# Reading the mixer's projection input as two runs of 128 tokens in turn

## The chip, the cores and the metric

The kernel runs on one core of one Trainium2 chip. A core has a matrix engine (TensorE, here PE, with its weight loads shown apart as PEld), a vector engine (VectorE, DVE), an activation engine (ScalarE, ACT), a general engine (GpSimd, POOL) and a queue engine that issues transfers (SyncE, SP). Each works through its own instructions in order. The metric is the device time of one execution in microseconds; lower is better. Three runs of the kernel before took 1980.0, 1980.95 and 1983.24 us, the median is 1980.95.

## What is computed

One decoder layer in float32 for 256 tokens of width 2048: a feed-forward block (SwiGLU, inner width 5632), a token mixer, a second feed-forward block, and a final norm. Each is normed and modulated by a conditioning vector. The change lies in the mixer, whose projection is one large product with `w_in`:

```python
def hybrid_mixer(h, w_in, w_out, ...):
    proj = (h @ w_in).astype(jnp.float32)
    q_f, k_f, v_f, f_f, qkv_g, a_g, b_g, z_g = jnp.split(proj, SPLIT_IDX, axis=-1)
    logf = jax.nn.log_sigmoid(f_f + fox_f_bias)            # forget gates
    o_f = forgetting_attention(heads(q_f), heads(k_f), heads(v_f), logf)
    qkv_g = jax.nn.silu(causal_dwconv(qkv_g, gdn_conv))    # 4 taps along the tokens
    q_g, k_g, v_g = jnp.split(qkv_g, 3, axis=-1)
    o_g = gated_delta_rule(l2norm(q_g), l2norm(k_g), v_g, g_log, beta)
    ...
    return o @ w_out
```

There are 8 heads of forgetting attention ("fox") and 8 heads of the gated delta rule ("gdn"), each of width 128.

## The kernel before

**Precision.** A float32 product is made of three faster ones: weights and activations are each split into a high part and a rest, and high x high, high x rest and rest x high are summed in PSUM. For weights, ACT casts the high part (`whi`, line 109) and DVE subtracts it from the raw block for the rest (`wlo`, line 121). Weights come in blocks of eight 128x128 tiles, 512 KB each, in the order of use (`Stream`, lines 84 to 130), with three buffers each for the raw block, `whi` and `wlo`. So the cast of a block waits until PE has done with the block three before it.

**Layout of the activations.** The normed input `hs` has, for each of 16 slices of 128 features, a rest and a high part of 256 tokens. Two views of it are used. `part` (line 331) is for the feed-forward blocks: tokens are stored as two runs (even and odd tokens, written through `pairs`), and the matmul reads one element of the one and one of the other run in turn, which gives the tokens in order. `plain` (line 329) is for the mixer: 256 tokens in order, contiguous. `woven` (line 74) is the helper that reads a contiguous stretch as two halves in turn.

**The mixer's projections.** `project` (line 717) makes one or several outputs of 128 features x 256 tokens. It runs over 16 slices and makes three matmuls for each weight tile (lines 725 to 727) with `plain` as the moving operand. There are 41 such outputs: one for the gates, 24 for gdn (keys, queries, values), 16 for fox queries and keys. `project_rows` (line 731) is another form, with the activations as the stationary operand, for the fox values and the output gate `z`.

**What reads the sums.** `gates` (line 755) copies 24 rows out of PSUM (758), and works out decays in steps: exponentials on ACT, a series on DVE, cumulative sums on PE (800 to 809), then a copy (811) and a transfer of the rows to memory, from which they are read again spread over the partitions. `conv_silu` (line 871) makes the four-tap convolution: tap 3 on ACT (874), the others on DVE (876), with the sums read from PSUM each time, then a SiLU on ACT (877). It runs 24 times, with temporary tiles from the tag `pt`, which has four buffers (line 418). The fox queries and keys are taken out of PSUM by ACT at line 1192.

**Order.** The per-head work (`keys`, `decays`, `solve`, `gdn`, `fox`, `to_out`) is written as generators, and `tick` (line 433) advances them between the weight tiles at due times. A scheduler then sets the order of the instructions on each engine from these, so an edit in one place can move others. The list `ORDER` (line 49) sets which head's projection comes when; the first call projects the gates and three key heads together.

Of the kernel before, what the change touches and what calls it, by code (L numbers as in the profile page):

```python
# [12 lines left out]
AF = mybir.ActivationFunctionType  # L13
ALU = mybir.AluOpType
# [4 lines left out]
T = 256  # L19
KD = D // P  # L20
# [6 lines left out]
HD = 128  # L27
# [46 lines left out]
def woven(ap):  # L74

    return ap.rearrange("p (a b) -> p b a", a=2)


def pairs(ap):

    return ap.rearrange("p (b a) -> p b a", a=2)


class Stream:
# [49 lines left out]
def layer_kernel(ctx: ExitStack, tc: tile.TileContext, xrow, c, adaw, cols, cst, w, out, order, dbg=None):  # L134
    nc = tc.nc
    V, A, G, PE = nc.vector, nc.scalar, nc.gpsimd, nc.tensor
# [21 lines left out]
    def psn(i, name):  # L158

        i %= 8  # L160
        return psb(name) if i < N_BIG else pss(name) if i < N_BIG + N_GDN else psf(name)
# [165 lines left out]
    LO, HI = 0, 1  # L327

    plain = hsf[:, : KD * HS].rearrange("p (k i) -> p k i", k=KD)[:, :, : 2 * T].rearrange("p k (q t) -> p k q t", q=2)
# [78 lines left out]
    def h_need(k):  # L408

        h_upto(k + AHEAD)  # L410
# [6 lines left out]
    def pt(name):  # L417
        return tmp.tile([P, T], F32, name=name, tag="pt", bufs=4)
# [14 lines left out]
    def tick(us):  # L433
        clock["now"] += us
        for kind in chains:
            if chains[kind] and clock["now"] >= due[kind]:
                advance(kind)
# [248 lines left out]
    def mixer():  # L686
# [12 lines left out]
        R = slice(0, GR)  # L699
# [17 lines left out]
        def project(items):  # L717

            pp = [psn(i, "pp") for i in range(len(items))]
            todo = [(i, k) for k in range(KD) for i in range(len(items))]  # L720
            for i, k in todo:
                m, n = items[i]
                h_need(k)
                wh, wl = W.next(m, k, n)
                PE.matmul(pp[i][:, :T], wh, plain[:, k, HI], start=(k == 0), stop=False)  # L725
                PE.matmul(pp[i][:, :T], wh, plain[:, k, LO], start=False, stop=False)  # L726
                PE.matmul(pp[i][:, :T], wl, plain[:, k, HI], start=False, stop=(k == KD - 1))  # L727
                tick(TILE_US)
            return [p_[:, :T] for p_ in pp]

# [24 lines left out]
        def gates(ps):  # L755

            yr = x[:, 8]
            A.copy(yr[R], ps[R])
            y, ny, e, em, t0, q = (x[:, j, : 2 * GR].rearrange("p (t r) -> p t r", t=2) for j in range(10, KD))
            coef = tiny.tile([P, GR + PAD["hid"]], F32, name="coef", bufs=1)[:, :GR]  # L760
            tc.keep_in_program_order(A.activation(coef, L("alog"), AF.Exp))
            V.tensor_scalar(coef, coef, -1.0, None, ALU.mult)
            yield 1.0
            pc = psf("pcol")
            pcv = pc[:, : 2 * GR].rearrange("p (t r) -> p t r", t=2)
            for t in range(2):
                PE.transpose(pcv[:, t], yr[R, t * P : (t + 1) * P], ident[R, :GR])
            both = lambda c_: c_.unsqueeze(1).to_broadcast([P, 2, GR])
            V.tensor_tensor(y, pcv, both(L("gbias")), ALU.add)
            V.tensor_tensor(y, y, both(C("sgn")), ALU.mult)  # L770
            V.scalar_tensor_tensor(ny, y, -1.0, y, ALU.mult, ALU.min)
            A.activation(e, ny, AF.Exp)
            V.tensor_scalar(em, y, 0.0, None, ALU.min)
            A.activation(em, em, AF.Exp)

            S = ny
            V.tensor_scalar(t0, e, 2.0, None, ALU.add)
            V.reciprocal(t0, t0)
            V.tensor_tensor(S, e, t0, ALU.mult)
            V.tensor_tensor(t0, S, S, ALU.mult)  # L780
            V.tensor_scalar(q, t0, 1.0 / 17.0, None, ALU.mult)
            for n in (15, 13, 11, 9, 7, 5, 3):
                V.scalar_tensor_tensor(q, q, 1.0 / n, t0, ALU.add, ALU.mult)
            V.scalar_tensor_tensor(q, q, 1.0, S, ALU.add, ALU.mult)
            V.tensor_scalar(y, y, 0.0, None, ALU.max)
            V.scalar_tensor_tensor(y, q, 2.0, y, ALU.mult, ALU.add)
            V.tensor_tensor(y, y, both(coef), ALU.mult)

            V.tensor_scalar(t0, e, 1.0, None, ALU.add)
            V.reciprocal(t0, t0)  # L790
            V.tensor_tensor(colS[:, :, 4], em[:, :, 16:24], t0[:, :, 16:24], ALU.mult)
            yield 6.0

            fox_, gdn_ = slice(0, NH), slice(NH, 2 * NH)
            pr = psf("prow")
            po = psf("pcum")
            pcs = po[:, : 6 * NH].rearrange("p (t q r) -> p t q r", t=2, q=3)
            for t in range(2):
                sl = slice(t * P, (t + 1) * P)
                PE.matmul(pr[:NH, T + t * P : T + (t + 1) * P], y[:, t, gdn_], C("tri64"), start=True, stop=True)  # L800
                PE.matmul(pr[:NH, sl], y[:, t, fox_], C("tri"), start=True, stop=(t == 0))
                if t:
                    PE.matmul(pr[:NH, sl], y[:, 0, fox_], L("ones"), start=False, stop=True)
            for t in range(2):
                PE.matmul(pcs[:, t, 1], C("tri64"), y[:, t, gdn_], start=True, stop=True)
                PE.matmul(pcs[:, t, 2], C("tru64"), y[:, t, gdn_], start=True, stop=True)
                PE.matmul(pcs[:, t, 0], C("tri"), y[:, t, fox_], start=True, stop=(t == 0))
                if t:
                    PE.matmul(pcs[:, t, 0], L("ones"), y[:, 0, fox_], start=False, stop=True)
            rt = x[:, 8:10].rearrange("p a t -> p (a t)")[:NH]  # L810
            A.copy(rt, pr[:NH])
            nc.sync.dma_start(rows, rt)
            V.tensor_copy(colS[:, :, 0:2], pcs[:, :, 0:2])
            A.activation(colS[:, :, 2:4], pcs[:, :, 1:3], AF.Exp)
            V.tensor_tensor(nbeg, colS[:, :, 4], colS[:, :, 2], ALU.mult)
            V.tensor_scalar(nbt, colS[:, :, 4], -1.0, None, ALU.mult)
            V.tensor_scalar(ng, colS[:, :, 1], -1.0, None, ALU.mult)
            yield 2.0
            fetch_rows(0)
            yield 1.0  # L820
# [48 lines left out]
            G.memset(t_, 0.0)  # L869

        def conv_silu(ps, n, dst):
            cv = pt("cv")
            tap = lambda s: L("conv", 4 * n + s, 1)
            A.activation(cv, ps, AF.Copy, scale=tap(3))
            for s in range(1, 4):
                V.scalar_tensor_tensor(cv[:, s:], ps[:, : T - s], tap(3 - s), cv[:, s:], ALU.mult, ALU.add)
            A.activation(dst, cv, AF.Silu)

        kk = {}
# [277 lines left out]
        def step(kind, h):  # L1157
            if kind == "K":
                have_keys(h, project([("qkv", NH + h)])[0])
            elif kind == "G":  # L1160
                rowg[h] = row_of(h, 1, "g")
                pq = project([("qkv", h)])[0]
                pv = project([("qkv", 2 * NH + h)])[0]
                finish("gdn", h - 3)
                finish("out", h - 3)
                finish("k", h // 4 * 4 + 3)
                qv[h] = otile("qv")
                conv_silu(pq, h, qv[h].bitcast(F32)[:, 0])
                conv_silu(pv, 2 * NH + h, qv[h].bitcast(F32)[:, 1])
                ups[h] = decay(h)  # L1170
                start("gdn", h, gdn(h))
            elif kind == "Z":
                if h:
                    finish("fox", 3)
                pz = project_rows("z", h)
                zss[h] = [spare(0), spare(2)] if h else [m1p.tile([P, 512], F32, name=f"zs{t}") for t in range(2)]
                for t in range(2):
                    A.activation(zss[h][t], pz[t], AF.Silu)
            elif kind == "V":
                if h:  # L1180
                    finish("k", NH)
                pv = project_rows("vf", h)
                vts[h] = [spare(4 * h), spare(4 * h + 2)]
                for t in range(2):
                    A.copy(vts[h][t], pv[t])
            else:
                rowf[h] = row_of(h, 0, "f")
                pp = [project([(m, h)])[0] for m in ("qf", "kf")]
                finish("fox", h - 1)
                qk = spare(8 + 2 * (h % 2)).rearrange("p (a t) -> p a t", a=2)  # L1190
                for i in range(2):
                    A.activation(qk[:, i], pp[i], AF.Copy, scale=1.0 / math.sqrt(HD) if i == 0 else 1.0)
                start("fox", h, fox(h, qk, vts[h // 4]))

        first = project([("gt", 0)] + [("qkv", NH + h) for h in range(3)])
# [168 lines left out]
```

## Time and profile before

| | |
|---|---|
| Median of three runs | 1980.95 us |
| Profiled execution | 1983.29 us |
| Span of its instructions | 1981.5 us |
| Mean granted TensorE clock | 0.991 |
| PE busy | 1919.3 us (97%) |
| DVE busy | 1582.2 us (80%) |
| ACT busy | 1045.7 us (53%) |
| Matmuls in `project` | 1968 (lines 725, 726, 727, 656 each) |
| First and last of them | from 753.3 to 1166.6 us |

All lines of the profile come from the one profiled execution. A row of a group has: line, engine, operation, output <- input, sizes, count | busy time in us, mean ns of one | idle time of its engine just before, and what ended most of it. A row of the timeline has the start in us, the duration in us, engine, line, operation, count, and in brackets the idle time before it with what ended that. Neighbouring instructions of one kind are merged there. A row of waits has: who waited, on whom: total us, times, longest. Matmuls overlap: the next one starts before the one before it has ended, so a sum of durations is more than the time they take.

### The profile page before, as it was taken

The numbers are of one execution on the slowest core, as the hardware profiler recorded it, in microseconds if no ns is written. First come the engines' busy times: TensorE is split into PE (matmuls) and PEld (weight loads), VectorE is DVE, ScalarE is ACT, GpSimd is POOL, SyncE is SP. The second block draws the span as 40 slices with busy tenths as digits, with TensorE's granted clock in tenths as the row PEclk, the third lists the DMA queues.
The fourth block names the chain that finished last, engine by engine and source line by source line (L and its number), as shares of the span: only waits on it lengthen the run. The fifth ranks groups of instructions, "written<-read, shape, count | busy, mean of one in ns | idle before, by whom it ended". The sixth has DMA issues, their size and how long they took to land.

```text
span 1981.5 us, 33632 instructions
## 1 busy us (share of the span) xinstructions
PE 1919.3 (97%) x13059; PEld 1783.2 (90%) x13059; DVE 1582.2 (80%) x2424; ACT 1045.7 (53%) x1607; POOL 64.2 (3%) x60
## 2 busy tenths in 40 slices
PE   8999999999999999999999999999999999999997
PEld 6999999988999988889989998989999999999996
DVE  6999988999999998879878879987677666666665
ACT  6544555433555447666656656565454445555442
POOL 0000000000000120000000002000000000000012
PEclk8999999999999999999999999999999999999998
DMA  9989867999999984776666658667777555555563
GB/s 341 350 329 333 297 213 261 393 376 382 355 343 359 340 328 173 248 237 230 210 240 241 210 213 308 234 222 251 250 240 258 203 202 198 204 200 200 201 200 117
DMA packets 129489, 519.56 MB, mean 262 GB/s; under 512 B 18217, under 2 KB 21545, under 8 KB 111153
## 3 DMA queue, kind: packets, MB, share of 16 engines
q1 hardware_dynamic: 129330, 517.42, 72.6%
q8 instruction: 102, 1.67, 0.3%
q14 instruction: 57, 0.47, 0.1%
HBM read 512.89 MB, written 4.47 MB: 261 GB/s over the span
## 4 chain that ended last, share of the span: by engine, by line
PE 66%; DVE 14%; DMA 10%; issue 6%; ACT 4%; SPq 0%; DVEq 0%; ACTq 0%
PE pd L455 12%; PE pg L451 9%; PE pu L451 9%; PE pd L456 6%; DVE wlo L121 6%; DMA adat<-in_ada_dram 5%; PE pu L452 5%; PE pg L452 5%; DMA wraw<-in_w_dram 4%; PE pgu L539 3%; PE pgu L538 3%; PE pgu L537 3%; PE pp L725 2%; PE pp L727 2%; PE pp L726 2%
## 5 line engine op out<-in xcount | busy, mean ns | idle before, releaser
L121 DVE TENSOR_TENSOR wlo<-wraw,whi 128x1024 fp32r<-128x1024 f32 x674 | 820.6, 1226 | 238.2 <-ACT whi L109 236.0
L109 ACT CAST whi<-wraw 128x1024 fp32r<-128x1024 f32 x674 | 699.5, 1047 | 507.0 <-DMA wraw<-in_w_dram 195.0
L455 PE MATMUL pd<-hid,whi 128*128 128x512 f32 x1408 | 462.1, 382 | 0.8 <-DVE hid L470 0.8
L456 PE MATMUL pd<-hid,wlo 128*128 128x256 f32 x1408 | 384.6, 273 | 3.0 <-DVE wlo L121 3.0
L242 DVE CUSTOM_DVE_ANT_0 adat<-adat,cs,colt 128x2048 f32<-128x2048 f32 x140 | 329.0, 2350 | 52.6 <-DMA adat<-in_ada_dram 52.2
L451 PE MATMUL pg<-hs,whi 128*128 128x512 f32 x912 | 303.8, 384 | 3.9 <-ACT whi L109 2.8
L451 PE MATMUL pu<-hs,whi 128*128 128x512 f32 x912 | 302.6, 382 | 0.0
L455 PEld LDWEIGHTS pd<-hid,whi 128*128 128x128 f32 x1408 | 266.0, 189 | 38.0 <-DVE hid L470 1.4
L456 PEld LDWEIGHTS pd<-hid,wlo 128*128 128x128 f32 x1408 | 270.5, 192 | 5.9 <-DVE wlo L121 5.7
L537 PE MATMUL pgu<-hs,whi 128*128 128x256 f32 x896 | 245.9, 277 | 8.4 <-ACT hs L341 6.7
L452 PE MATMUL pu<-hs,wlo 128*128 128x256 f32 x912 | 249.9, 274 | 0.5 <-DVE wlo L121 0.3
L452 PE MATMUL pg<-hs,wlo 128*128 128x256 f32 x912 | 249.6, 274 | 0.0
L539 PE MATMUL pgu<-hs,wlo 128*128 128x256 f32 x896 | 244.6, 277 | 3.6 <-DVE wlo L121 3.5
L538 PE MATMUL pgu<-hs,whi 128*128 128x256 f32 x896 | 245.9, 276 | 0.1
L451 PEld LDWEIGHTS pg<-hs,whi 128*128 128x128 f32 x912 | 173.2, 190 | 28.6 <-issue 3.0
L725 PE MATMUL pp<-hs,whi 128*128 128x256 f32 x656 | 189.9, 291 | 4.2 <-ACT whi L109 1.4
L451 PEld LDWEIGHTS pu<-hs,whi 128*128 128x128 f32 x912 | 172.4, 189 | 23.6
L727 PE MATMUL pp<-hs,wlo 128*128 128x256 f32 x656 | 186.8, 286 | 1.6 <-DVE wlo L121 1.6
L726 PE MATMUL pp<-hs,whi 128*128 128x256 f32 x656 | 186.2, 284 | 0.0
L537 PEld LDWEIGHTS pgu<-hs,whi 128*128 128x128 f32 x896 | 172.4, 193 | 9.6 <-ACT hs L341 7.1
L452 PEld LDWEIGHTS pu<-hs,wlo 128*128 128x128 f32 x912 | 175.2, 192 | 3.2 <-DVE wlo L121 2.6
L452 PEld LDWEIGHTS pg<-hs,wlo 128*128 128x128 f32 x912 | 176.0, 193 | 0.4
(334 smaller groups left out, 2629.9 us busy)
## 6 DMA issues: line engine op xcount, KB each, us to landing
wraw<-in_w_dram SPq DMA_DIRECT2D x674, 512.0 KB, 4.5
adat<-in_ada_dram SPq DMA_DIRECT2D x140, 1024.0 KB, 7.3
xr<-in_xr_dram SPq DMA_DIRECT2D x4, 512.0 KB, 6.3
adaf<-in_ada_dram SPq DMA_DIRECT2D x4, 512.0 KB, 8.6
adaf<-in_ada_dram SPq DMA_DIRECT2D x2, 1024.0 KB, 12.2
xd<-x SPq DMA_DIRECT2D x4, 512.0 KB, 8.3
rw<-rowd SPq DMA_DIRECT2D x16, 128.0 KB, 6.4
x<-xd SPq DMA_DIRECT2D x4, 512.0 KB, 8.5
```

What stands on the lines that cost most here:

```text
L109: self.cast = self.nc.scalar.copy(self.h, r).ins
L121: nc.vector.tensor_tensor(self.l, r, self.h.bitcast(F32), ALU.subtract)
L242: V.tensor_tensor_reduce(t, t, cs, 1.0, L("adab", q, 1), ALU.mult, ALU.add, mod[:, q : q + 1])
L451: PE.matmul(ps, wt[0], both, start=(k == 0), stop=False)
L452: PE.matmul(ps[:, T:], wt[1], part(k, HI), start=False, stop=(k == KD - 1))
L455: PE.matmul(ps, wt[0], act.rearrange("p q (a b) -> p q b a", a=2), start=first, stop=False)
L456: PE.matmul(ps[:, :T], wt[1], woven(act[:, 0]), start=False, stop=last)
L537: PE.matmul(o, wh, part(k, HI), start=first and s == 0, stop=False, skip_group_check=skip)
L538: PE.matmul(o, wh, part(k, LO), start=False, stop=False, skip_group_check=skip)
L539: PE.matmul(o, wl, part(k, HI), start=False, stop=last, skip_group_check=skip)
L725: PE.matmul(pp[i][:, :T], wh, plain[:, k, HI], start=(k == 0), stop=False)
L727: PE.matmul(pp[i][:, :T], wl, plain[:, k, HI], start=False, stop=(k == KD - 1))
```

## The change

`project` reads its input through `woven`: the two halves of 128 tokens in turn (token 0, 128, 1, 129 and so on). The sums stand in PSUM in that order. ACT puts them back as it takes them out: the new `turns` reads PSUM with a step of two elements, first the even and then the odd positions, and `runs` writes them as two runs of 128. `conv_silu` gets a copy for that (`cp`), in SBUF, and its four taps read the copy instead of PSUM. The gates' copy and the evacuation of the fox queries and keys keep their instruction and get the two views. `project_rows` is as before.

```diff
+def runs(ap):
+    return ap.rearrange("p (a b) -> p a b", a=2)
+
+def turns(ap):
+    return ap.rearrange("p (b a) -> p a b", a=2)
...
-                PE.matmul(pp[i][:, :T], wh, plain[:, k, HI], start=(k == 0), stop=False)
-                PE.matmul(pp[i][:, :T], wh, plain[:, k, LO], start=False, stop=False)
-                PE.matmul(pp[i][:, :T], wl, plain[:, k, HI], start=False, stop=(k == KD - 1))
+                hh, hl = woven(plain[:, k, HI]), woven(plain[:, k, LO])
+                PE.matmul(pp[i][:, :T], wh, hh, start=(k == 0), stop=False)
+                PE.matmul(pp[i][:, :T], wh, hl, start=False, stop=False)
+                PE.matmul(pp[i][:, :T], wl, hh, start=False, stop=(k == KD - 1))
...
-            A.copy(yr[R], ps[R])
+            A.copy(runs(yr[R]), turns(ps[R]))
...
         def conv_silu(ps, n, dst):
-            cv = pt("cv")
+            cp, cv = pt("cp"), pt("cv")
             tap = lambda s: L("conv", 4 * n + s, 1)
-            A.activation(cv, ps, AF.Copy, scale=tap(3))
+            A.copy(runs(cp), turns(ps))
+            A.activation(cv, cp, AF.Copy, scale=tap(3))
             for s in range(1, 4):
-                V.scalar_tensor_tensor(cv[:, s:], ps[:, : T - s], tap(3 - s), cv[:, s:], ALU.mult, ALU.add)
+                V.scalar_tensor_tensor(cv[:, s:], cp[:, : T - s], tap(3 - s), cv[:, s:], ALU.mult, ALU.add)
             A.activation(dst, cv, AF.Silu)
...
-                    A.activation(qk[:, i], pp[i], AF.Copy, scale=1.0 / math.sqrt(HD) if i == 0 else 1.0)
+                    A.activation(runs(qk[:, i]), turns(pp[i]), AF.Copy, scale=1.0 / math.sqrt(HD) if i == 0 else 1.0)
```

The order of the instructions is made anew for the changed kernel, and around the first key heads it differs from the order before.

## The prediction

> **What bounds the kernel now.** I read the page's busy shares first, then the busy time by stretch, then the mixer's groups, then the starts of single matmuls, and last the waits.
>
> ```profile
> PE 1919.3 (97%) x13059; PEld 1783.2 (90%) x13059; DVE 1582.2 (80%) x2424; ACT 1045.7 (53%) x1607; POOL 64.2 (3%) x60
> ```
>
> TensorE (PE) is nearly always busy. Whether that also holds where the change sits is told by the stretches of the mixer. Columns: stretch, its length, then busy time of PE, weight loads, DVE, ACT and POOL, then granted clock, DMA share, GB/s.
>
> ```profile
> 753.00:800.00 47.00, 45.54 (x365) 44.41 (x366) 39.20 (x95) 36.15 (x70) 0.42 (x2) 0.96 0.50 175
> 800.00:900.00 100.00, 93.84 (x608) 83.56 (x607) 82.97 (x196) 66.84 (x130) 0.42 (x2) 1.00 0.72 246
> 900.00:1167.00 267.00, 261.99 (x2022) 249.87 (x2022) 224.40 (x526) 165.01 (x352) 0.00 (x0) 1.00 0.63 221
> ```
>
> The same view for the instructions on `pp`, the tile that `project` sums into:
>
> ```profile
> 753.00:800.00 47.00, 42.21 (x331) 41.04 (x332) 6.54 (x15) 2.37 (x6) 0.96 0.50 175
> 800.00:900.00 100.00, 40.91 (x318) 38.35 (x317) 7.14 (x15) 3.19 (x7) 1.00 0.72 246
> 900.00:1167.00 267.00, 179.94 (x1323) 162.56 (x1322) 19.97 (x42) 11.42 (x27) 1.00 0.63 221
> ```
>
> So PE sets the pace after 900 us (98% busy, 1323 of the 1968 matmuls), DVE following at 84% (224.40 of 267). Between 800 and 900 PE is idle for 6.2 us.
>
> **The removed time: the spacing of the matmuls.**
>
> ```profile
> L725 PE MATMUL pp<-hs,whi 128*128 128x256 f32 x656 | 189.9, 291 | 4.2 <-ACT whi L109 1.4
> ...
> L727 PE MATMUL pp<-hs,wlo 128*128 128x256 f32 x656 | 186.8, 286 | 1.6 <-DVE wlo L121 1.6
> L726 PE MATMUL pp<-hs,whi 128*128 128x256 f32 x656 | 186.2, 284 | 0.0
> ```
>
> A matmul's duration includes its overlap with the next one, so what counts is the distance between starts. In `project`, which reads 256 tokens in one contiguous run:
>
> ```profile
> 901.05 0.28 PE L727 MATMUL pp<-hs,wlo 128*128 128x256 f32 x1
> ...
> 903.15 0.28 PE L727 MATMUL pp<-hs,wlo 128*128 128x256 f32 x1
> ```
>
> There are 18 steps between these two: 2.10 / 18 = 116.7 ns. The first FFN has the same three 256-token products for each weight tile, but its input is read as two runs in turn (`part`, 576 bytes apart):
>
> ```profile
> 252.10 0.28 PE L537 MATMUL pgu<-hs,whi 128*128 128x256 f32 x1
> ...
> 254.56 0.28 PE L538 MATMUL pgu<-hs,whi 128*128 128x256 f32 x1
> ```
>
> 22 steps, 2.46 / 22 = 111.8 ns (the clock after 900 us is full too, 1.00 above, so the clock is not the cause). Where a 512-token and a 256-token product alternate, again in turns:
>
> ```profile
> 1700.07 0.27 PE L452 MATMUL pu<-hs,wlo 128*128 128x256 f32 x1
> ...
> 1702.69 0.27 PE L452 MATMUL pu<-hs,wlo 128*128 128x256 f32 x1
> ```
>
> Eight pairs in 2.62 us, or 327.5 ns for 768 columns, 109.2 ns for each 256. The changed `project` has the form of the first FFN, so I take 111.8: a gain of 4.9 ns for each of 3 x 656 = 1968 matmuls, 9.6 us in all. Bounds: nothing (if the extra belongs to this stage, not to the reading order) and 7.5 ns, 14.8 us.
>
> [...]
>
> How much of the 9.6 us reaches the end? After 900 us: 1323 x 4.9 = 6.5 us, of which I count 5.5, because DVE would then be busy for 224.40 of some 261 us, and its bursts already make PE wait now and then. From 800 to 900: 318 x 4.9 = 1.6 us; I count 0.8, since this stretch also waits for weights:
>
> ```profile
> ACT whi L109 <- PE pp L726: 32.0, 28, 2.4
> ACT whi L109 <- DMA wraw<-in_w_dram: 27.0, 17, 4.7
> PE pv L738 <- DVE cv L876: 1.6, 1, 1.6
> PE pp L725 <- ACT whi L109: 1.4, 2, 0.9
> ```
>
> (waits from 753 to 1167 us: total, times, longest). From 753 to 800: 331 x 4.9 = 1.6 us, of which 1.0 before the first group of four projections ends. Together 7.3 us.
>
> **The added and moved work.** Each of the 24 calls of `conv_silu` gets one ACT copy (`cp`) that reads PSUM with a step of two elements; no row shows that form. The evacuations of fox queries and keys and of the gates take the same pattern (16 + 1).
>
> ```profile
> L462 ACT COPY mg<-pg 128x256 f32<-128x256 f32 x57 | 20.9, 367 | 24.6 <-PE pg L452 24.6
> L874 ACT ACTIVATE cv<-pp,colt 128x256 f32<-128x256 f32 x24 | 11.0, 466 | 1.5 <-PE pp L727 1.5
> L1092 ACT ACTIVATE oh<-pft,colt 128x256 fp32r<-128x256 f32 x8 | 5.8, 730 | 7.6 <-PE pft L1142 7.5
> L876 DVE SCALAR_TENSOR_TENSOR cv<-pp,colt,cv 128x255 f32<-128x255 f32 x24 | 11.2, 472 | 1.3 <-ACT cv L874 1.2
> L338 DVE SCALAR_TENSOR_TENSOR ht<-x,g,nrow 128x256 f32<-128x256 f32 x48 | 22.0, 477 | 0.7 <-ACT nrow L668 0.3
> L877 ACT ACT_TABLE_LOAD x11 | 14.1, 1283 | 1.3 <-DVE cv L876 1.1
> ```
>
> A plain copy out of PSUM takes 367 ns, one whose output is woven 730. The new one writes two long runs, so I take 0.4 us: 24 x 0.4 = 9.6 us of ACT time, 17.5 at the upper bound. ACT is busy for 165.01 of 267 us after 900; there this lies beside PE. The taps on DVE read `cp` in SBUF in place of PSUM: 477 against 472 ns, no change. One gain: the copy frees the PSUM bank at once, before the three taps; the wait of `pv` for `cv` above (1.6 us on PE) goes, and I count 1.0.
>
> The head of the mixer pays. `cp` and `cv` now share the four buffers of tag `pt`, so only two convolutions can be under way, and the changed order on ACT shows it: copies, taps and SiLUs of the first three key heads alternate with the gates' exponentials, and ACT reloads its table for each switch, four loads more in the whole kernel (36 for 32), all here. In the kernel before, PE makes the gates' cumulative sums (L800 to L809) in the middle of the third further key projection, and six casts of weights (L109) stand on ACT between the gates' copy (L758) and the copy of these sums (L811). In the changed order the sums come right after the second, and only two casts stand ahead of their copy.
>
> ```profile
> 778.37 0.36 ACT L758 COPY x<-pp 24x256 f32<-24x256 f32 x1
> ...
> 784.65 1.28 ACT L772 ACT_TABLE_LOAD   x1
> ...
> 796.43 0.56 ACT L811 COPY x<-prow 8x512 f32<-8x512 f32 x1
> ```
> ```profile
> 778.78 0.38 PE L725 MATMUL pp<-hs,whi 128*128 128x256 f32 x1 [0.91 <-ACT x L758]
> ...
> 794.94 0.39 PE L800 MATMUL prow<-cstt,x 128*8 128x128 f32 x2
> ...
> 797.49 0.37 PE L809 MATMUL pcum<-x,colt 128*128 128x8 f32 x2
> ```
>
> By hand, in the new order. ACT, from 778.4: gates' copy 0.3, `cp` 0.4, table 1.28, `coef` 0.1, `cv` 0.4, `cp` 0.4, cast 1.0, `cv` 0.4, cast 1.0, table 1.28, SiLU 0.4, `cp` 0.4, table 1.28: the first exponential starts at 787.0. In the profile it started at 785.9 (784.65 + 1.28) and the sums 9.0 us later, at 794.94, in which DVE also made three `wlo` of 1.2 us that now stand ahead: 5.4 us are left, so 792.4. PE starts the first of the two projections at 778.8 and has their four blocks of 24 matmuls done after 96 x 0.112 = 10.7 us; with the key transposes behind them it is at the sums near 790.4 and waits 2.0 us. The sums take 2.8 us (794.94 to 797.7); after the first 1.2 of these ACT copies the rows (0.3), makes a `cp` (0.4) and the next cast (1.0), to 795.3, and DVE its `wlo` (1.2), to 796.5. PE, done with the sums at 795.2, makes two matmuls and waits for `wlo` about 1.1 us. Together 3.1, of which some 0.3 stood there before: 2.8 us lost. Bounds: 0 (the rows leave for memory 3 us earlier, which `decays` may use) and 6 (the four table loads of 1.283 us end to end, and the rest).
>
> **Sum.** 7.3 + 1.0 - 2.8 = 5.5 us off the span of 1981.5, or 1976.0. The profiled execution took 1983.29 us in all, 2.3 above the runs' median of 1980.95, so I take the 5.5 off the median: 1975.5.
>
> **The rivals.**
> - Everything comes through: 109.2 ns as in the alternating products, all of 14.8 us, bank gain 1.6, head 2.8: 13.6 off, 1967. For it: PE is 98% busy. Against: 111.8 in the place with three 256-token products. 13%.
> - DVE, at 84% and in turn with ACT, takes half of the gain: 3.7 + 1.0 - 2.8, so 1979. For it: wlo and the chains share DVE in order. Against: only 1.4 us of PE waits for `whi` at L725 in the whole mixer. 12%.
> - The change doesn't do what it says: the 116.7 belongs to the mixer (its chains' traffic), not to the reading order. Then 0 + 1.0 - 2.8: 1983. For it: no row shows the same stage read both ways. Against: the 18 steps quoted have no chain work of PE among them, and are long all the same. 12%.
> - Slower: ACT's queue becomes the pace of the weight stream. Each convolution makes ACT wait, in order, for three taps (3 x 0.472 = 1.4 us) before the SiLU or the next copy, plus 0.3 us more of its own work, and the casts stand behind it. A cast now waits for PE 1.1 us on the mean (32.0 / 28); beyond that the delay reaches PE. It decides from 1.1 us for each convolution: 24 x (1.7 - 1.1) = 14 us lost, the head among it, less 7.3 gained: 1988. Against: the wait for the taps exists today too and costs PE little. 15%.
> - The plain store read in turns is slow, the gain mirrored: 1968 x 4.9 = 9.6 us lost, with head and bank 11.4: 1992. 3%. [...]
>
> **How the numbers follow.** The forecast, 1975.5, has the remaining 45%, with its own range from 1970 to 1979. This kernel's measurement tells 0.2%, 4 us, from no change: faster is below 1977, slower above 1985. Faster: most of the forecast and all of the first rival, 0.54. Same: the second and third rivals and the rest of the forecast's range, 0.25. Slower: the last two and the tail of the third, 0.21. Leaving a tenth out at each end, the range goes from 1966, just under the first rival, to 1987, short of the slow case.
>
> **What would show it.** Right: starts on `pp` 111 to 113 ns apart; the `cp` copies near 0.4 us; the end of the last projection some 5 us earlier and everything after it unchanged; the wait of `pv` for `cv` gone. For the head: gaps on PE right before and right after the gates' sums. Wrong: starts still 116 apart (third rival), PE waiting on `whi` more than 10 us over the mixer (fourth), or `cp` near 0.7 us with casts late behind it.

## The result, and the profile after

The changed kernel takes 1994.18 us (median of 5 runs, 1994.07 to 2002.7) beside 1980.95 for the kernel before in 5 runs on the same chip: a ratio of 1.0066, 95% interval 1.0048 to 1.0084. It is slower by 13 us, where 5.5 us less was forecast. Its profiled execution took 1994.51 us, with a span of 1992.7.

PE is busy for 1920.8 us in all, where it was 1919.3, though the matmuls of the projections now start closer together (111.8 ns apart instead of 116.7, below). The stretches of the mixer, in the same cut as before the change:

```profile
753.00:800.00 47.00, 41.87 (x337) 40.44 (x337) 38.78 (x93) 35.43 (x62) 0.42 (x2) 0.92 0.45 158
800.00:900.00 100.00, 89.58 (x543) 77.91 (x542) 78.82 (x178) 69.08 (x139) 0.42 (x2) 0.95 0.67 233
900.00:1167.00 267.00, 255.92 (x2010) 241.99 (x2009) 224.94 (x525) 168.53 (x363) 0.00 (x0) 1.00 0.63 223
```

PE is idle for 10.4 us between 800 and 900, where it was 6.2, and the granted clock there is 0.95 instead of 1.00. Some 4 us of the difference at 753 are older than the mixer: the first FFN, whose code is the same, ended later in this execution. Over all the kernels below, which have the same first FFN, the first matmul of the projections starts anywhere from 752.0 to 757.3 us, and the fastest of them starts at 757.1: this is not the change. So the stage is best measured by itself, from its first to its last matmul. The view of the instructions on `pp` and on `pv` (count, shortest/median/longest in ns, first to last start) gives that. Before:

```profile
L725 PE MATMUL pp<-hs,whi x656: 274/280/580, 753.3 to 1166.3; 128*128 128x256 f32 x164
L738 PE MATMUL pv<-whi,hs x128: 377/379/567, 813.9 to 1037.0; 128*128 128x512 f32 x128
```

And after:

```profile
L736 PE MATMUL pp<-hs,whi x656: 273/275/581, 757.3 to 1180.1; 128*128 128x256 f32 x164
L749 PE MATMUL pv<-whi,hs x128: 379/379/634, 821.8 to 1051.8; 128*128 128x512 f32 x128
```

The projections lasted 413.0 us and now last 422.8, which is 9.8 us more. (The spans of the two executions differ by 11.2 us: 4.0 stand ahead of the stage, 9.8 in it, and 2.6 come back behind it.) From the first `pp` to the first `pv`, which I call the head, it was 60.6 us and is now 64.5; from there to the end 352.4, now 358.3.

Yet the two things that the change does directly came out as forecast. The timeline of PE, inside a run of 18 matmuls of one projection:

```profile
898.76 0.28 PE L738 MATMUL pp<-hs,wlo 128*128 128x256 f32 x1
...
900.66 0.28 PE L737 MATMUL pp<-hs,whi 128*128 128x256 f32 x1
```

17 steps in 1.90 us, or 111.8 ns, where it was 116.7. And the groups of instructions have the copies out of PSUM:

```profile
L885 ACT COPY cp<-pp 128x256 f32<-128x256 f32 x24 | 8.8, 365 | 0.6 <-PE pp L738 0.6
```

365 ns each: these copies, which read PSUM with a step of two elements, take what the plain copy of 367 ns does.

What is different is ACT's order in the head. The timeline of ACT, of which I show the table loads and the three steps to which the prediction gave times:

```profile
780.20 0.36 ACT L769 COPY x<-pp 24x256 f32<-24x256 f32 x1
...
780.84 1.28 ACT L772 ACT_TABLE_LOAD   x1
...
785.33 1.28 ACT L889 ACT_TABLE_LOAD   x1
...
787.32 1.28 ACT L783 ACT_TABLE_LOAD   x1
788.62 0.24 ACT L783 ACTIVATE x<-x 128x48 f32<-128x48 f32 x1
788.88 1.28 ACT L889 ACT_TABLE_LOAD   x1
...
791.01 1.28 ACT L785 ACT_TABLE_LOAD   x1
...
792.82 1.28 ACT L889 ACT_TABLE_LOAD   x1
...
795.06 0.58 ACT L822 COPY x<-prow 8x512 f32<-8x512 f32 x1
...
798.34 1.28 ACT L825 ACT_TABLE_LOAD   x1
...
804.37 1.28 ACT L889 ACT_TABLE_LOAD   x1
...
807.35 1.28 ACT L872 ACT_TABLE_LOAD   x1
...
809.07 1.28 ACT L889 ACT_TABLE_LOAD   x1
...
810.78 1.28 ACT L872 ACT_TABLE_LOAD   x1
```

L889 is the SiLU of `conv_silu`; L772, L783, L785, L825 and L872 are exponentials. They take turns, and every turn in these rows is a load of 1.28 us. With the one at 819.8 us there are 12 loads from 777 to 825 us; the kernel before has 8 there. Casts of weights stand behind them in the same queue. The groups of ACT in that stretch, before:

```profile
L109 ACT CAST whi<-wraw 128x1024 fp32r<-128x1024 f32 x14 | 14.4, 1053 | 12.1 <-DMA wraw<-in_w_dram 9.2 <-PE pp L726 2.9
```

and after:

```profile
L119 ACT CAST whi<-wraw 128x1024 fp32r<-128x1024 f32 x11 | 11.4, 1056 | 3.1 <-DMA wraw<-in_w_dram 2.5 <-PE pp L737 0.4
```

Three casts fewer in the same 48 us (11 also from 781 to 829 us, which allows for the later start), and their idle time, once 12.1 us, is 3.1: ACT has little room left, busy for 43.28 of the 48 us where it was 38.47. What that costs PE is seen in its waits for weights from 777 to 900 us (who waited, on whom: total, times, longest). Before:

```profile
PE pp L725 <- ACT whi L109: 1.4, 2, 0.9
PE pp L727 <- DVE wlo L121: 1.0, 2, 0.8
PE pv L739 <- DVE wlo L121: 0.4, 1, 0.4
```

After, with the one new wait beside them (`Ln` comes out of an exponential of the head, L872):

```profile
PE pv L750 <- DVE wlo L131: 4.1, 2, 2.5
PE pp L738 <- DVE wlo L131: 2.4, 2, 1.6
PE pk L901 <- DVE Ln L914: 2.0, 1, 2.0
PE pp L736 <- ACT whi L119: 1.7, 3, 1.1
PE pv L749 <- ACT whi L119: 0.7, 1, 0.7
```

DVE makes `wlo` out of `whi`, so both stand behind the cast: 2.8 us of waits for weights have become 8.9. Not all of that is the cast's own lateness: of the waits for `wlo`, one of 1.6 us ends at 837.8, where DVE makes a product of 2.3 us (`adat`, L252) just ahead of it, and the one that ends at 799.0 has two taps of a convolution ahead of it on DVE. The busy time by stretch of the head and of what follows, before:

```profile
777.00:825.00 48.00, 46.40 (x350) 43.52 (x349) 40.13 (x106) 38.47 (x81) 0.00 (x0) 1.00 0.58 200
825.00:900.00 75.00, 69.26 (x439) 60.73 (x438) 62.57 (x148) 49.01 (x90) 0.42 (x2) 1.00 0.75 256
```

After:

```profile
777.00:825.00 48.00, 42.79 (x335) 40.32 (x334) 38.55 (x100) 43.28 (x88) 0.00 (x0) 0.93 0.46 157
825.00:900.00 75.00, 67.29 (x382) 57.05 (x381) 58.06 (x124) 45.16 (x82) 0.42 (x2) 0.98 0.72 254
```

PE's idle time over the two stretches was (48 - 46.40) + (75 - 69.26) = 7.3 us and is 12.9: 5.6 us more. And the clock that was full is 0.93 and 0.98: 48 x 0.07 + 75 x 0.02 = 4.9 us of full-speed time not granted. Together 10.5 us, near the 9.8 by which the stage grew. That is not yet the whole account: after 900 us PE is idle for 11.1 of 267 us, where it was 5.0, and the shorter matmuls give about as much back (over the stage PE is busy for 399.2 us, with some 5 us more held back by the clock, where it was 401.4).

### The profile page after: what moved, and what is told of

Its sections match the earlier page's. It is cut to its first block, busy times and chain, and to the rows that moved or that the text cites. A ratio compares the mean times of both kernels' runs of the same rounds, so it can differ in the third digit from the quotient of the medians.

```text
span 1992.7 us, 33667 instructions
## 1 busy us (share of the span) xinstructions
PE 1920.8 (96%) x13058; PEld 1782.6 (89%) x13059; DVE 1587.2 (80%) x2424; ACT 1058.6 (53%) x1635; POOL 64.3 (3%) x60
## 4 chain that ended last, share of the span: by engine, by line
PE 66%; DVE 15%; DMA 9%; issue 5%; ACT 5%; SPq 0%; DVEq 0%; ACTq 0%
PE pd L465 14%; PE pg L461 9%; PE pu L461 9%; PE pd L466 7%; DVE wlo L131 6%; DMA adat<-in_ada_dram 5%; PE pu L462 5%; PE pg L462 5%; DMA wraw<-in_w_dram 3%; PE pgu L549 3%; PE pgu L547 3%; PE pgu L548 3%; DVE adat L252 2%; ACT whi L119 2%; PE po L465 2%
## 5 line engine op out<-in xcount | busy, mean ns | idle before, releaser
L252 DVE CUSTOM_DVE_ANT_0 adat<-adat,cs,colt 128x2048 f32<-128x2048 f32 x140 | 329.0, 2350 | 49.0 <-DMA adat<-in_ada_dram 48.4
L549 PEld LDWEIGHTS pgu<-hs,wlo 128*128 128x128 f32 x896 | 172.7, 195 | 5.8 <-DVE wlo L131 5.8
## 6 DMA issues: line engine op xcount, KB each, us to landing
adaf<-in_ada_dram SPq DMA_DIRECT2D x2, 1024.0 KB, 12.1
```

Of the source, the lines that this page charges most:

```text
L252: V.tensor_tensor_reduce(t, t, cs, 1.0, L("adab", q, 1), ALU.mult, ALU.add, mod[:, q : q + 1])
L549: PE.matmul(o, wl, part(k, HI), start=False, stop=last, skip_group_check=skip)
```

## The experiments

In the table, the head and the whole of the projections are worked out from the starts in the view of `pp` and `pv` as above (one profiled execution each). "Lost" is PE's idle time from 777 to 900 us and, behind the plus, the time that the clock held back there, both as above. Ratios are to the kernel before on the same chip; the rows come from several chips, so two of them are compared by their ratios and not by their times.

| kernel | us | ratio, 95% interval | loads, 777-825 | head / projections, us | lost, us |
|---|---|---|---|---|---|
| before | 1980.95 | 1 | 8 | 60.6 / 413.0 | 7.3 + 0 |
| changed | 1994.18 | 1.0066 (1.0048-1.0084) | 12 | 64.5 / 422.8 | 12.9 + 4.9 |
| e1 read only | 1982.61 | 0.999 (0.9973-1.0007) | 8 | 60.5 / 411.6 | 7.4 + 1.5 |
| e2 copy only | 1999.05 | 1.0067 (1.0044-1.0091) | 12 | 65.6 / 424.7 | 13.4 + 3.4 |
| e3 copy elsewhere | 2000.35 | 1.0079 (1.0053-1.0104) | 10 | 68.9 / 426.4 | 16.0 + 5.3 |
| e4 woven convolution | 1977.35 | 0.9971 (0.9955-0.9988) | 8 | 59.2 / 407.4 | 9.4 + 0 |
| f1 exponentials held | 1983.38 | 1.0001 (0.9983-1.0019) | 8 | 60.5 / 414.4 | 10.4 + 1.5 |
| f2 copies in main loop | 1982.95 | 1.0 (0.9984-1.0016) | 8 | 57.9 / 414.6 | 8.5 + 3.8 |
| f3 copies in head | 1985.49 | 1.0013 (0.9998-1.0028) | 12 | 67.4 / 418.9 | 12.4 + 7.1 |
| f4 before, 0.335 | 1980.93 | 0.9987 (0.9973-1.0001) | 8 | 59.1 / 408.3 | 5.8 + 0 |
| g1 before, alternating | 1996.73 | 1.0076 (1.0063-1.0089) | 12 | 67.6 / 429.3 | 14.5 + 8.5 |
| g2 read only, 0.335 | 1976.58 | 0.9974 (0.9963-0.9985) | 8 | 60.7 / 410.7 | 9.8 + 0 |
| g3 woven convolution, 0.335 | 1971.79 | 0.9955 (0.9942-0.9967) | 8 | 57.1 / 400.8 | 7.0 + 0 |
| h1 copies, held, 0.335 | 1980.26 | 0.999 (0.9977-1.0002) | 8 | 62.8 / 411.0 | 10.7 + 3.4 |

**First set: which part of the change loses the time.** e1 has the new reading and nothing else; the sums are used in PSUM's order, so the tokens stay exchanged.

```diff
-                PE.matmul(pp[i][:, :T], wh, plain[:, k, HI], start=(k == 0), stop=False)
+                hh, hl = woven(plain[:, k, HI]), woven(plain[:, k, LO])
+                PE.matmul(pp[i][:, :T], wh, hh, start=(k == 0), stop=False)
```

> Only the reading order is changed: project reads in turns, and the sums are left in that order (no copy cp, no reordering), so the mixer works on permuted tokens. Theory A (spacing is a real gain of 4.9 ns for each of 1968 matmuls, the loss comes with the copy): starts 112 ns apart and 1971 to 1975 us. Theory B (something else paces the mixer, shorter spacing reaches the end hardly at all): 112 ns apart, but 1978 to 1982 us. Theory C (most of the loss lies outside the mixer, in the first FFN, where the changed kernel was 4 us later): the first FFN is late here too, 1978 or more.

e2 has the old reading and the copy, here a plain one, ahead of each convolution:

```diff
+            A.copy(cp, ps)
-            A.activation(cv, ps, AF.Copy, scale=tap(3))
+            A.activation(cv, cp, AF.Copy, scale=tap(3))
```

> Only the extra copy cp in conv_silu, plain, with the input read contiguously as before. Theory A: the head of the mixer (weight casts 264 to 284) loses 10 us as in the changed kernel, and the spacing gains nothing: 1994 to 2002 us. Theory B: the copy is what there is to see, spacing neither gains nor loses: 1992 to 1996. If the strided reading of PSUM were the cost, this one stays near 1982.

e3 is the changed kernel with 16 of the 24 `cp` (keys and queries, not values) moved out of the four shared buffers, into a half of the result's tile that is written later:

```diff
-            conv_silu(ps, NH + h, kk[h].bitcast(F32)[:, 0])
+            conv_silu(ps, NH + h, kk[h].bitcast(F32)[:, 0], kk[h].bitcast(F32)[:, 1])
```

> The changed kernel, with cp of the keys and gdn queries put in the unused half of their output tile, so that cp and cv no longer share the four buffers of pt. Theory A1 (the four buffers force the alternation of copies, SiLUs and exponentials): the head loses at most 4 us, 1978 to 1985 us. Theory A2 (the additional hop on ACT itself and the order made for it): 1989 to 1995 us. The built order has 34 table loads on ACT, against 32 before and 36 in the changed kernel; by loads alone at 1.28 us it would be 2 to 3 us under the changed kernel, 1991.

e4 has the new reading without any copy: the taps work in PSUM's order, where one token back is two elements back, 72 small operations on DVE mend the seam between the two halves, and the SiLU puts the result in order.

```diff
-            A.copy(runs(cp), turns(ps))
+            A.activation(cv, ps, AF.Copy, scale=tap(3))
             for s in range(1, 4):
+                V.scalar_tensor_tensor(cv[:, 2 * s :], ps[:, : T - 2 * s], tap(3 - s), cv[:, 2 * s :], ALU.mult, ALU.add)
+                o = cv[:, 1 : 2 * s : 2]
+                V.scalar_tensor_tensor(o, ps[:, T - 2 * s : T : 2], tap(3 - s), o, ALU.mult, ALU.add)
+            A.activation(runs(dst), turns(cv), AF.Silu)
```

> The change without the copy: the convolution works in PSUM's order of tokens (a tap of s tokens is a shift of 2s positions, and a small extra DVE operation of s elements for the tokens at the seam of the two runs), and the SiLU puts the tokens back. 72 more DVE operations of about 0.15 us, 11 us of DVE in the mixer. Theory A: 32 table loads, head as before, gain of the spacing kept: 1972 to 1978 us. Theory B (DVE or the weight stream paces the mixer): 1980 to 1988 us.

The copy alone (e2), with the order that it brings, makes the whole loss: 1.0067 beside the changed kernel's 1.0066, within the range of theory A. The reading alone (e1) gains 0.1%, 2 us, and its interval includes no change. Its time of 1982.61 lies just above the range of theory B, and its projections start at 753.9 us, so theory C, a late first FFN, is out. The sharing of the four buffers is not needed for the loss: with other room for most copies the loss is no smaller (e3, which stands above both of its ranges and 9 us above the count by loads). And e4, which keeps the reading and drops the copy, is faster than both kernels, within the range of theory A.

**Second set: is it the copies, or the order that they bring about?** f1 is the changed kernel, copies and all; the two exponentials of the gates are held behind the third key's SiLU.

```diff
+            with tc.issue_after(last_silu[NH + 2]):
+                A.activation(e, ny, AF.Exp)
...
+            last_silu[n] = A.activation(dst, cv, AF.Silu).ins
```

> The changed kernel, copies and all, with one thing held back: the two gate exponentials of the mixer's head may not be issued before the SiLU of the third key projection. ACT's table loads in the whole kernel fall back from 36 to the 32 of the kernel before. Theory H (the copies cost nothing where they stand; they shift the order on ACT in the head so that SiLU and exponential alternate there, each turn with a table load of 1.28 us, and the queue of casts behind them is late by 10 to 11 us): the loss goes, 1981 to 1986. Theory C (each of the 24 copies costs its 0.36 us and its place in ACT's queue, wherever it stands): the loss stays, 1991 to 1997. Between the two, 1987 to 1990, both would hold a share.

f2 and f3 split the copies: f2 has e4's convolution for the keys and the copy for queries and values, f3 the other way round.

```diff
-            conv_silu(ps, NH + h, kk[h].bitcast(F32)[:, 0])
+            conv_woven(ps, NH + h, kk[h].bitcast(F32)[:, 0])
...
-                conv_silu(pq, h, qv[h].bitcast(F32)[:, 0])
+                conv_copy(pq, h, qv[h].bitcast(F32)[:, 0])
```

> The woven reading everywhere; the copy only behind the projections of the main loop (the values' and gates' side), while the key projections of the head do without it (their convolution works in the order of PSUM). 32 table loads. Theory H: the copies of the main loop are free, so it stands with the kernel that has no copy at all (1977 there): 1976 to 1982. Theory C: most of the copies are still there, so most of the loss too: 1986 to 1994.

> The other half: copies only behind the key projections of the head, none in the main loop. 36 table loads. Theory H: the whole loss, 1990 to 1998, with 6 or more us more from the gates' copy to the first matmul of the products with the values' weights (35.1 us in the kernel before). Theory C: a few copies only, 1979 to 1985.

f4 changes one figure of the planner in the kernel before:

```diff
-TILE_US = 0.35
+TILE_US = 0.335
```

> The kernel before, with its plain reading and no copy; only the planner's figure for the length of a projection's tile is set to 0.335 us. Its order of ACT's work in the head then has 36 table loads instead of 32, as the changed kernel's has. Theory H: slower by the loads and by what waits behind them, 1986 to 1996, with neither a copy nor a woven read in it. Theory C: within a few us of the kernel before, 1977 to 1984.

f1 takes the loss away with all 24 copies in place: 1.0001. Its busy time by stretch:

```profile
777.00:825.00 48.00, 43.97 (x347) 41.22 (x346) 41.12 (x102) 40.77 (x88) 0.00 (x0) 1.00 0.56 196
825.00:900.00 75.00, 68.62 (x423) 59.77 (x421) 61.33 (x148) 48.02 (x89) 0.42 (x2) 0.98 0.71 249
```

347 matmuls in the head instead of 335, the clock full there, 196 GB/s instead of 157. f2 has no loss against the kernel before, with the copies in the main loop alone. It is above its range by 1 us all the same, and above e4, which has the same head, by 0.29% or 5.7 us. f3 fell short of its expectation, 1985.49 where 1990 to 1998 stood. That expectation forgot where the kernel starts from: outside the head f3 is e4, and e4 is 0.29% under the kernel before. Against e4 it is slower by 0.42%, 8.3 us, and its projections are longer by 418.9 - 407.4 = 11.5 us. From the gates' copy to the first `pv` it takes 41.3 us (819.4 - 778.1), as the changed kernel does (41.6), where the kernel before takes 35.5.

e4, f2, f3 and the changed kernel form a square: the reading is the same in all, and the copy stands nowhere, in the main loop, behind the keys, or in both. The copies of the main loop cost 0.29% where the head has the old order (f2 beside e4) and 0.53%, 10.5 us, where it has the new one (changed beside f3); the copies behind the keys, with the order that they bring, cost 0.42% (f3 beside e4) and 0.66% (changed beside f2). By the intervals in the table such a difference is good to about 0.23% either way (an estimate). So the main loop has a share of its own. But what stands in place of the copy here is the woven convolution, which is faster than e1's plain one by 0.19% for a reason that the runs don't show; beside e1, which has the plain convolution and no copy, f1 with all its copies is slower by 0.11% only, which is within the noise.

f4 did not test what it was meant to: it has 36 loads in all, but the extra four came after 860 us, and its head has the old order. With them it is no slower than the kernel before, so four loads more in another place cost nothing that shows, unless the new figure gains by itself what they cost. It stays as the control for the third set.

**Third set: the order without a copy, and the lost spacing.** g1 is the kernel before, with its plain reading and no copy. Two exponentials of one column are added behind the first two key SiLUs, on a tile whose content is used up, and the SiLU that comes next is held behind each.

```diff
             A.activation(dst, cv, AF.Silu)
+            if n in (NH, NH + 1):
+                with tc.issue_after(si):
+                    held["at"] = A.activation(cv[:, :1], cv[:, :1], AF.Exp).ins
```

> The kernel before, plain reading and no copy, with two tiny exponentials added in the head (one column, in place, of a tile whose content is already used up), one behind the SiLU of the first key projection and one behind that of the second, ahead of the next SiLU. They force the alternation of SiLU and exponential on ACT that the changed kernel has in its head: 12 table loads there instead of 8, 36 in all. Theory H2 (four loads of 1.28 us and the casts behind them are what the head lost, the copies only brought the order about): 8 or more us of the 11 lost, 1988 to 1994, and about 40 us from the gates' copy to the first matmul of the products with the values' weights (35.1 before, 41.6 changed). Theory C2 (ACT can bear the loads alone, and the 8 copies beside them make the loss): 1980 to 1986, and 35 to 37 us there.

g2 and g3 are e1 and e4 with the planner's figure of f4.

> The reading in turns alone (no copy, the sums left in PSUM's order), with the planner's figure for three matmuls set to 0.335 us, which is 3 x 111.7 ns, instead of 0.35. Theory S (the spacing's gain is lost because the planner, counting in the old length, sets the steps of the attention where their inputs are not ready, so PE waits): 1976 to 1979.5, and PE's idle time from 900 to 1165 us falls back from 8.9 us toward the 4.9 of the kernel before. Theory B (ACT, DVE and the weight stream set the pace there, PE has time to spare either way): 1981 to 1985, and the idle time stays at 8 to 10 us.

> The fastest kernel so far (the reading in turns, the convolution worked in PSUM's order, no copy; 1977.35) with the same figure of 0.335 us. Theory S: another 2 to 5 us off, 1972 to 1976. Theory B: no gain, 1976 to 1981.

g1 loses 0.76%, as much as the changed kernel or more, with no copy and no woven read in it; its time, 1996.73, is above the 1988 to 1994 of theory H2, and it takes 42.1 us from the gates' copy to the first `pv` (35.5 before). The two added instructions are short themselves, as the groups of ACT from 777 to 825 us show:

```profile
L883 ACT ACTIVATE cv<-cv 128x1 f32<-128x1 f32 x2 | 0.4, 195 | 0.0
```

The stretches of g1 have the same marks as the changed kernel's, only deeper:

```profile
777.00:825.00 48.00, 41.63 (x299) 39.38 (x298) 35.45 (x96) 41.10 (x82) 0.00 (x0) 0.87 0.37 136
825.00:900.00 75.00, 66.92 (x372) 57.37 (x371) 58.15 (x125) 42.14 (x75) 0.42 (x2) 0.97 0.68 243
```

Idle (48 - 41.63) + (75 - 66.92) = 14.5 us, 7.1 more than before; held back by the clock 8.5; together 15.6, and its projections are 16.3 us longer than before. So f1 and g1 show the part of the order from both sides: without the alternation the loss is gone, though all copies stay, and the alternation without a copy costs as much as the change does. PE's waits for `whi` and `wlo` from 753 to 1185 us go with it: 2.9 to 5.5 us in the nine kernels with 8 loads in the head, 7.3 to 13.7 in the five with 10 or 12. That the copies are free is not shown by this; the square above speaks against it. Open as well is how the loss divides inside the order. Four loads are 5.1 us of ACT, g1 loses three times that; and e3, with 10 loads, loses as much as the kernels with 12. So the number of loads isn't the whole measure: which casts and inputs stand behind them counts as well, and the runs don't take these apart.

For the spacing, theory S had the times about right (1976.58 within 1976 to 1979.5, 1971.79 just under 1972 to 1976), but its mechanism isn't borne out. f4 is the reason: the plain kernel, whose matmuls still start 116.7 ns apart, gains from the new figure too. The figure is worth 0.13% without the new reading (f4 beside 1), 0.16% with it (g2 beside e1), 0.16% with the woven convolution (g3 beside e4), 0.11% with the copies (h1 beside f1): 2.2 to 3.2 us each time, none of them clear of the noise by itself, but all four on the same side. It makes a better order of its own, and it isn't the key to the spacing. PE's idle time from 900 to 1165 us, which S wanted to fall back, went from e1's 8.9 to 10.0 in g2. The reading itself gains the same in either order: 0.10% (e1 beside the kernel before) and 0.13% (g2 beside f4), 2 to 2.6 us, again each within the noise.

Where the rest of the spacing went is seen in the busy time from 900 us on. Before:

```profile
900.00:1165.00 265.00, 260.12 (x2010) 248.26 (x2009) 223.08 (x521) 164.57 (x351) 0.00 (x0) 1.00 0.62 221
```

and e1:

```profile
900.00:1165.00 265.00, 256.09 (x2017) 242.84 (x2015) 223.66 (x524) 164.30 (x351) 0.00 (x0) 1.00 0.63 222
```

In the same 265 us PE does nearly the same number of matmuls, and 4.0 us of what it saves it now stands idle. For whom, its waits from 900 to 1165 us say (total, times, longest). Before:

```profile
PE pvq L968 <- ACT qv L877: 1.8, 3, 1.1
PE pp L725 <- DVE Z L982: 0.8, 1, 0.8
PE pft L1142 <- DVE on L1138: 0.8, 2, 0.4
```

and e1:

```profile
PE pvq L969 <- ACT qv L878: 3.0, 4, 1.5
PE pft L1143 <- DVE on L1139: 1.6, 3, 0.7
PE pp L726 <- DVE cv L877: 1.3, 1, 1.3
PE po L1054 <- DVE st L1065: 0.9, 1, 0.9
```

Most of these are steps of the two attentions: PE comes to them sooner, and their inputs from ACT and DVE do not. Whether DVE's pace or the order behind it sets that is not settled, as g2 does not tell it.

**Last.** h1 puts both edits on the changed kernel: f1's hold and f4's figure.

> The changed kernel with all its copies and two lines beside them: the gate exponentials held behind the third key's SiLU (as in the run that stood at 1983.4) and the planner's figure for three matmuls set to 0.335 us. If both causes are named rightly (the order on ACT in the head, and the steps of the attention planned in the old length), the change with its copies comes under the kernel before: 1974 to 1980. If the copies of the main loop take the spacing's gain themselves: 1981 to 1986, as without the new figure.

It stands at 1980.26, between the two ranges that were expected, and at 0.999 (0.9977 to 1.0002): level with the kernel before, perhaps a little under it, and 0.76% or 15 us under the changed kernel. It does not decide between its two cases. g3 is the best of all, 9 us under the kernel before, with the reading of the change and without its copy. That g3 and e4 gain more than the reading's 2 us is measured and not explained: e4 beside e1 is 0.19% and so is g3 beside g2, although e4 and g3 have 72 operations more on DVE.

## Why the prediction was wrong, step by step

- **Spacing of the matmuls, 111.8 ns:** right, 111.8. The rival by which it belongs to the mixer is out, and so is the mirrored one: the reading in turns is the fast one here, 111.8 beside 116.7 ns for the plain reading.
- **What of it reaches the end, 7.3 us:** mis-sized. e1 and g2 have 2 to 2.6 us, and no interval tells e1's gain from none. I took off 1.0 us after 900 us for DVE's bursts; the idle time of PE took four times that. The second rival (DVE takes half) came nearer on this term.
- **The copy, 0.4 us and beside PE:** right for its length (0.365). That it lies beside PE in the main loop and costs nothing is not borne out: f1, with all copies and the old head, is 2 us over e1, which has none, within the noise, but f2 is 5.7 us over e4 and the changed kernel 10.5 us over f3. The term was put at nothing; the runs leave it between about 2 and 10 us, and do not show by which wait it would reach PE.
- **The bank, 1.0 us:** the wait of `pv` for `cv` is gone, as forecast. No run had it alone, so its size stays open.
- **The head, 2.8 us with bounds of 0 and 6:** this is the step that failed. The changed kernel beside f1, which differs by the hold alone, is 0.65% slower: 12.9 us; by the square it is 8.3 to 13.1. The count by hand was good as far as it went: I had the first exponential 8.6 us after the gates' copy and it came after 8.4 (788.62 - 780.20); I had PE at a stand for 3.1 us around the gates' sums, and the three gaps there were 0.65, 0.22 and 1.62 us, 2.5 together (0.65 where I had 2.0, and 1.84 where I had 1.1, so that the sum is near by some luck):

```profile
793.76 0.39 PE L811 MATMUL prow<-cstt,x 128*8 128x128 f32 x2 [0.65 <-DVE x L798]
...
796.90 0.38 PE L736 MATMUL pp<-hs,whi 128*128 128x256 f32 x1 [0.22 <-ACT whi L119]
...
799.01 0.38 PE L738 MATMUL pp<-hs,wlo 128*128 128x256 f32 x1 [1.62 <-DVE wlo L131]
```

  But I stopped at 797 us, when ACT had caught up with the sums, and even my upper bound of 6 priced the four extra loads end to end and nothing that waits behind them. Only two of them lie ahead of the copy of the sums: six loads stand between the gates' copy and the copy of the sums, where there were four. The other two lie in the alternation from 804 to 811 us that I had not followed, and they pushed the casts back further: by 825 us three are missing, and PE waits for weights for 8.9 us in place of 2.8. The second part of the failure is the clock, which I took as 1.00 throughout and which was 0.93 from 777 to 825 us and 0.98 from there to 900.
- **The sum.** By ratios against the kernel before: reading -2.0 (e1), copies in the old order +2.2 (f1 beside e1), the order of the head (changed beside f1) +12.9. These add up to the whole, 13.1 us or 0.66%, by the way they are taken; what the runs say is how it is shared out, and another way through them shares it otherwise: from e4 the copies behind the keys with their order make 8.3 us and those of the main loop 10.5 more, out of 18.8.
- **The slower rival** was on the right side, with ACT's queue as the cause, but at another place. It saw a toll on each of 24 convolutions, decided by casts that come late for PE. Its sign, more than 10 us of waits on `whi` over the mixer, did not come by the letter: there are 2.4 us, and 7.2 more on the `wlo` that is made from it, 9.6 in place of 3.4. But nearly all of that, 8.9 us, stands between 777 and 900 us, and f2, with 16 copies in the main loop and the old order in the head, has 4.3 in all: the weights come late in the head, and not at each convolution.
- **The range.** It was to leave out a tenth at each end. The last two rivals stood at 1988 and 1992 with 18% together, all above its end of 1987, so the upper end was too low by the prediction's own chances; the measured 1994 lies above both of these rivals too.

## What to carry to other kernels

An instruction that is cheap and looks well hidden (here 24 copies of 365 ns) may still be dear through the order that a scheduler makes around it (1.0066 with the new order of the head, 1.0001 with the exponentials held): compare the two orders on the engine's queue, count what changes sides (here SiLU and exponential, at 1.283 us a turn), and follow the count until the engine has idle time again, not until the first wait is met. A dearer order can be tried in a kernel without the change, and a better one in the kernel with it; the two runs together tell the part from its side effect. And a gain on an engine that is 98% busy need not be worth its full length, if that engine meets chains from others right behind it: in e1 PE stood idle for 4.0 us of what it saved from 900 to 1165 us, and the kernel gained 2 us, within the noise.

## What the runs showed of the hardware

In the changed kernel the profile has the granted clock at a half for three stretches of 3.413 us between 777 and 900 us, from 799.28, 816.35 and 874.37 us on. Each stands right behind a stretch of that length in which PE was idle for 1.5 to 2.7 us. The busy time around the first of them, and below it a stretch of the same length that was as empty and had no such sequel (columns as above, the granted clock after POOL):

```profile
795.87:799.28 3.41, 1.57 (x12) 1.29 (x12) 2.24 (x5) 2.33 (x4) 0.00 (x0) 1.00 0.03 5
799.28:802.69 3.41, 3.41 (x18) 3.41 (x18) 2.56 (x5) 3.40 (x10) 0.00 (x0) 0.50 0.80 259
963.12:966.53 3.41, 1.62 (x16) 1.43 (x14) 3.35 (x8) 1.18 (x5) 0.00 (x0) 1.00 0.00 0
966.53:969.95 3.41, 3.41 (x33) 3.41 (x32) 2.69 (x6) 1.75 (x5) 0.00 (x0) 1.00 0.62 210
```

PE was busy for 1.57 of 3.41 us in the stretch ahead of the first half clock, for 1.92 ahead of the second and for 0.70 ahead of the third; each took up to 1.7 us of full-speed time right behind the wait. In these rows a half clock stands behind a stretch that was 46% busy, and none behind another that was 47% busy. Which gaps bring the half clock is not settled by these runs. In the kernel before, the clock stays at 1.00 from 777 to 900 us.
